# Weight-block sums of a seven-product feed-forward layer on GpSimd, result sums 512 wide

## The chip, the cores and the metric

The kernel runs on one core of a Trainium2 chip. The metric is the device time of one execution in microseconds. One core has TensorE (PE, with PEld for its weight loads), VectorE (DVE), ScalarE (ACT), GpSimd (POOL) and SyncE (SP, here the issuer of most DMAs). A comparison takes the median of several executions; the profile is one execution.

## The reference, cut to what matters

A two-layer decoder on 512 tokens of width 1024: each layer has a feed-forward block, a token mixer (latent attention in layer 0, sparse attention in layer 1) with memory attention, and a second feed-forward block, each followed by a layer norm. The change touches the four feed-forward blocks alone:

```python
D_MODEL, SEQ, D_FF = 1024, 512, 2816

def swiglu(x, w_gu, w_down):
    g, u = jnp.split(x @ w_gu, 2, axis=-1)
    return (jax.nn.silu(g) * u) @ w_down

x = layer_norm(DN_ALPHA * x + 0.5 * swiglu(x, ffn_w_gu[layer, 0], ffn_w_down[layer, 0]),
               ln_g[layer, 0], ln_b[layer, 0])
```

## The kernel before

**Arithmetic.** Every matrix product is made with float32r operands split in two: `split` (L195) casts a tile to hi on ACT (L199) and makes lo = source - hi on DVE (L200). A product is then hi x hi, hi x lo and lo x hi, so three matmuls stand for one.

**A feed-forward block** (`ffn`, L457) has 22 blocks of 128 hidden features, in five groups of four or five (`GROUPS`). An "s" is a single: gate and up are made plainly (`single`, two weight units). A "d" is a pair of gate and up made together by `seven` (L485): gate half and up half of the weights are each cut in two along the input features, the tokens in two halves of 256, and the 2 x 2 by 2 x 2 block product is made with seven quarter products instead of eight. There are 77 pairs in the four blocks (19, 19, 20 and 19). A quarter (L371) is 12 matmuls of 128x256: four hi x hi (L376), four hi x lo (L377), four lo x hi (L380).

**Weight units.** `_unit_order` lists the order in which weight tiles are used; a pair takes four units, g0 to g3, and behind each group come its down-projection units, one per hidden block. `prep` (L154) loads a unit through SP (`load`, L127) into one of four `wraw` buffers and splits it into one of seven hi/lo slots (three of `wring`, four of `W.extra`). For a pair `combined` (L133) loads only g0 (the gate weights) and g1 (the up weights, U) and makes the other operands by four 128x512 sums: two for g1 (L145, L146), one for g2 (L149), one for g3 (L151), each in place or into a third buffer. `unit` prepares up to four units ahead in program order.

**Token forms.** The quarters multiply not only token blocks but differences of them, `F.t[1]` to `F.t[4]`, made once per block by `token_forms` (L386) from raw copies b.

**Result sums.** A pair's seven quarter results lie in four PSUM banks: p12, p45, p67 and p3. One ACT copy (L495) and seven DVE sums of 128x256 (L496, L505 to L509, L513) make the gate half gs and the up half us; `evac` (L471) then takes silu on ACT, the product with 0.5 and up on DVE (L474) and the split into hhi and hlo. PSUM has eight banks, which `fbank` deals out in turn, so a bank comes round again two pairs later.

**Down projection.** `by_units` (L438) runs a group's units over two token tiles and then over the other two; it starts on the banks that have been free longest. The last group of a block goes through `token_major` (L421) instead, token tile 0 to 3 on banks 0,1 to 6,7, with residual sum (L315) and layer norm (L319) behind each tile; the norm takes its power on POOL (L328).

**What sets the order.** The program is written as a dataflow; a planner places each engine's instructions by priority and estimated time before the run, so an engine's order need not be that of the code, and it is fixed when the kernel runs. Each engine takes its instructions in that order and waits at semaphores.

Of the kernel before, what the change touches and what calls it, by code (L numbers as in the profile page):

```python
# [9 lines left out]
F32 = mybir.dt.float32  # L10
# [7 lines left out]
P = 128  # L18
# [86 lines left out]
def tile_trunk(ctx: ExitStack, tc, a: dict, out):  # L105
# [27 lines left out]
    def combined(name, idx):  # L133


        l, f, m = idx
        lo, up = slice(0, 512), slice(512, 1024)
        op = nc.vector.tensor_tensor
        if name == "g0":
            W.g = load(a["gu"][l, f, m, 0])  # L140
            return W.g
        if name == "g1":
            W.u = load(a["gu"][l, f, m, 1])
            W.s = wraw.tile([P, 1024], F32, name="wraw")
            op(W.s[:, up], W.g[:, lo], W.u[:, lo], op=ALU.subtract)  # L145
            op(W.u[:, lo], W.u[:, lo], W.u[:, up], op=ALU.add)  # L146
            return W.u
        if name == "g2":
            op(W.s[:, lo], W.u[:, lo], W.g[:, lo], op=ALU.subtract)  # L149
            return W.s  # L150
        op(W.g[:, up], W.g[:, up], W.s[:, lo], op=ALU.subtract)  # L151
        return W.g[:, up]

    def prep():  # L154
# [22 lines left out]
    def unit(name, idx, look):  # L177
        assert order[W.pos][:2] == (name, tuple(idx)), (order[W.pos], name, idx)
        if W.done <= W.pos:
            prep()  # L180
        ahead(look)
        W.pos += 1
        return W.ready.pop(W.pos - 1)
# [79 lines left out]
    def open_f(scope):  # L263
        F.st = ExitStack()
        W.extra = F.st.enter_context(tc.tile_pool(name=f"wx{scope}", bufs=NEXTRA, reuse_waits="tile"))
        F.xp = F.st.enter_context(tc.tile_pool(name=f"xp{scope}", bufs=1, reuse_waits="tile"))
        F.xp.tile([P, 112], F32, name="offset")
        F.sm = F.st.enter_context(tc.tile_pool(name=f"sm{scope}", bufs=2, reuse_waits="tile"))
        F.x = [F.xp.tile([P, D], F32, name=f"x{t}") for t in range(NT)]
        F.bk = 0  # L270
        W.scope = scope
        W.count = 0
        F.fst = ExitStack()
        F.fm = F.fst.enter_context(tc.tile_pool(name=f"fm{scope}", bufs=1, reuse_waits="tile"))
        for i in (1, 2, 3, 0, 4):
            for e in "hl":
                if i:
                    F.fm.tile([P, 4, 256], F32, tag=f"t{i}{e}", name="place")
            if not i:
                F.fm.tile([P, 80], F32, name="offset")  # L280
# [104 lines left out]

    def token_forms():  # L386

        def less(x, y):
            u = wraw.tile([P, 1024], F32, name="wraw").rearrange("p (k q) -> p k q", k=4)
            nc.vector.tensor_tensor(u, x, y, op=ALU.subtract)  # L390
            return u

        def form(i, u):
            F.t[i] = [F.fm.tile([P, 4, 256], F32R, tag=f"t{i}{e}", name="t") for e in "hl"]
            split(*F.t[i], u)

        b, F.t = F.raw, {}
        u = less(b[0, 1], b[0, 0])
        form(1, u)
        yield  # L400
        u = less(b[1, 1], u)
        form(2, u)
        yield
        u = less(u, b[1, 0])
        form(4, u)
        u = less(b[1, 1], b[0, 1])
        form(3, u)

    def prod(ps, w, a, first, last):
        (hi, lo), (ahi, alo), (p0, p1) = w, a, ps  # L410
# [46 lines left out]
    def ffn(l, f, i, halves, spill=None, final=False, mid=None, hook=None):  # L457
        hst, hp = right_pool(f"h{l}{f}")
        if hook is None:
            load_gb(l, i)  # L460
        groups = _groups(l, f)
        for gi, (m0, items) in enumerate(groups):
            n = len(items)
            hhi = hp.tile([P, 5, T], F32R, tag="hhi", name="hhi")
            hlo = hp.tile([P, 5, T], F32R, tag="hlo", name="hlo")

            def fbank():
                F.bk += 1
                return bank(F.bk - 1)

            def evac(j, pg, pu, sg=None):  # L471
                sg = sg or hp.tile([P, T], F32, tag="sg", name="sg", bufs=3)
                nc.scalar.activation(sg, pg, AF.Silu)
                nc.vector.scalar_tensor_tensor(sg, sg, 0.5, pu, op0=ALU.mult, op1=ALU.mult)  # L474
                split(hhi[:, j, :], hlo[:, j, :], sg)

            def single(j):
                pp = []
                for g in range(2):
                    w = unit("gu", (l, f, m0 + j, g), 4)  # L480
                    pp.append(fbank())
                    feature_major(w, pp[g], 0, T)
                evac(j, *pp)

            def seven(j):  # L485

                c0, c1 = slice(0, 256), slice(256, 512)
                gs = hp.tile([P, T], F32, tag="sg", name="gs", bufs=3)
                us = hp.tile([P, T], F32, tag="sg", name="us", bufs=3)
                op = nc.vector.tensor_tensor  # L490
                w = unit("g0", (l, f, m0 + j), 4)
                p12 = fbank()
                quarter(p12[:, c0], w, 0, *quarters(0, 0))
                quarter(p12[:, c1], w, 512, *quarters(1, 0))
                nc.scalar.copy(us[:, c0], p12[:, c0])  # L495
                op(gs[:, c0], us[:, c0], p12[:, c1], op=ALU.add)  # L496
                w = unit("g1", (l, f, m0 + j), 4)
                p45 = fbank()
                quarter(p45[:, c0], w, 512, *F.t[4])
                quarter(p45[:, c1], w, 0, *F.t[1])  # L500
                w = unit("g2", (l, f, m0 + j), 4)
                p67 = fbank()
                quarter(p67[:, c0], w, 0, *F.t[2])
                quarter(p67[:, c1], w, 512, *F.t[3])
                op(us[:, c0], us[:, c0], p67[:, c0], op=ALU.add)  # L505
                op(gs[:, c1], us[:, c0], p45[:, c1], op=ALU.add)
                op(us[:, c0], us[:, c0], p67[:, c1], op=ALU.add)
                op(us[:, c1], us[:, c0], p45[:, c1], op=ALU.add)
                op(us[:, c0], us[:, c0], p45[:, c0], op=ALU.subtract)  # L509
                w = unit("g3", (l, f, m0 + j), 4)  # L510
                p3 = fbank()
                quarter(p3[:, c0], w, 0, *quarters(1, 1))
                op(gs[:, c1], gs[:, c1], p3[:, c0], op=ALU.add)  # L513
                evac(j, gs, us, gs)

            j = 0
            if gi == 0:
                forms = token_forms() if halves else F.forms
            if gi == 0 and halves:
                ws, ps = [], []  # L520
                for j in range(3):
                    for g in range(2):
                        ws.append(unit("gu", (l, f, m0 + j, g), 0))
                        ps.append(fbank())
                if hook is not None:
                    hook()
                    load_gb(l, i, nc.sync)
                for c in range(2):
                    for w, p in zip(ws, ps):
                        feature_major(w, p, c * 256, c * 256 + 256)  # L530
                for j in range(3):
                    next(forms, None)
                    evac(j, ps[2 * j], ps[2 * j + 1])
                j = 3
                items = items[3:]
            for it in items:
                if gi == 0:
                    next(forms, None)
                if it == "d":
                    if gi == 0:  # L540
                        for _ in forms:
                            pass
                    seven(j)
                else:
                    single(j)
                j += 1

            last = gi == len(groups) - 1
            if gi == 2 and mid is not None:
                mid()  # L550

            def on_tile(t, ps):
                st = residual(t, ps, gi == 0, last)
                if last:
                    if t == 0 and not final:
                        new_xt()
                        if spill is None:
                            new_blocks()
                    norm_tile(t, st, spill, final)

            names = [("dn", (l, f, m0 + j)) for j in range(n)]

            def lhs(k, t):
                return hhi[:, k, t * P:(t + 1) * P], hlo[:, k, t * P:(t + 1) * P]

            if last:
                token_major(names, lhs, on_tile)
            else:
                by_units(names, lhs, on_tile, F.bk, 4)
        hst.close()  # L570
# [942 lines left out]
```

## Time and profile before

| what | value |
|---|---|
| median of 3 runs | 1869.84 us (1868.44 to 1870.9) |
| the profiled execution | 1869.39 us |
| its span, first to last instruction | 1867.5 us |
| PE, DVE, ACT, POOL busy | 1842.7, 1465.6, 869.4, 164.3 us |
| mean granted TensorE clock | 0.997 of full speed |

The span is 1.9 us shorter than the execution's own time. Busy PE means that a matmul is recorded as running; matmuls are pipelined, and the time of one as listed overlaps that of the next, so the pitch from start to start is what counts. The four feed-forward blocks lie at about 5 to 336, 568 to 880, 954 to 1267 and 1524 to 1852 us.

### The profile page before, as it was taken

How to read it: one execution, taken by the hardware profiler on the slowest of the kernel's cores; microseconds unless marked ns; L12 is line 12 of the kernel's file. 1: busy time of each engine (PE TensorE's matmuls, PEld its weight loads, DVE VectorE, ACT ScalarE, POOL GpSimd, SP SyncE). 2: the span in 40 equal slices, each digit the busy share in tenths (PEclk: the TensorE clock that was granted, in tenths of full speed). 3: DMA queues.
4: the chain of work that ended last, by engine and by line, in shares of the span. 5: the costliest groups of instructions: out<-in, count | busy, mean ns of one | idle time of the engine just before them, and what ended most of it. 6: DMA issues, size and time to landing. Idle time of an engine off the chain costs nothing.

```text
span 1867.5 us, 31922 instructions
## 1 busy us (share of the span) xinstructions
PE 1842.7 (99%) x12776; PEld 1651.6 (88%) x12776; DVE 1465.6 (78%) x2362; ACT 869.4 (47%) x1435; POOL 164.3 (9%) x185
## 2 busy tenths in 40 slices
PE   9999999999999999999999999999999999999998
PEld 8899899896679899899998998998956689999997
DVE  8798789757668789788897987987677378888887
ACT  6344345456545345334653443444566345434432
POOL 0000000025500000000100000001265100000000
PEclk9999999999999999999999999999999999999999
DMA  6333335531134234234333323343321224323322
GB/s 241 112 114 111 116 105 157 173 102 35 57 113 136 80 102 136 80 102 147 130 127 104 125 91 103 112 138 140 108 46 28 98 77 143 103 90 114 115 81 77
DMA packets 59701, 203.86 MB, mean 109 GB/s; under 512 B 6944, under 2 KB 7216, under 8 KB 59552
## 3 DMA queue, kind: packets, MB, share of 16 engines
q1 hardware_dynamic: 56848, 194.18, 31.8%
q0 software_dynamic: 2416, 7.11, 1.2%
q8 instruction: 101, 1.65, 0.4%
q10 hardware_dynamic: 288, 0.52, 0.1%
q14 instruction: 48, 0.39, 0.1%
HBM read 188.16 MB, written 7.34 MB: 105 GB/s over the span
## 4 chain that ended last, share of the span: by engine, by line
PE 89%; DVE 4%; ACT 2%; issue 2%; POOL 1%; DMA 1%; POOLq 0%; DVEq 0%; ACTq 0%
PE bank L376 13%; PE bank L380 13%; PE bank L377 13%; PE bank L415 4%; PE bank L411 4%; PE bank L413 4%; PE bank L412 4%; PE bank L414 4%; PE bank L416 4%; PE o L646 3%; PE bank L365 3%; PE bank L368 3%; PE bank L363 3%; PE tb L618 3%; PE s L1191 1%
## 5 line engine op out<-in xcount | busy, mean ns | idle before, releaser
L199 ACT CAST whi<-wraw 128x1024 fp32r<-128x1024 f32 (+3 forms) x479 | 463.4, 976 | 547.5 <-PE bank L416 246.9
L200 DVE TENSOR_TENSOR wlo<-wraw,whi 128x1024 fp32r<-128x1024 f32 (+3 forms) x479 | 536.4, 1126 | 133.7 <-ACT whi L199 132.7
L376 PE MATMUL bank<-t,whi 128*128 128x256 f32 x1232 | 298.4, 278 | 0.0
L377 PE MATMUL bank<-t,whi 128*128 128x256 f32 x1232 | 297.9, 278 | 0.0
L377 PEld LDWEIGHTS bank<-t,whi 128*128 128x128 f32 x1232 | 231.9, 188 | 0.0
L376 PEld LDWEIGHTS bank<-t,whi 128*128 128x128 f32 x1232 | 231.8, 188 | 0.0
L376 PE MATMUL bank<-xhi,whi 128*128 128x256 f32 x924 | 221.9, 277 | 0.0
L377 PE MATMUL bank<-xlo,whi 128*128 128x256 f32 x924 | 221.9, 277 | 0.0
L380 PE MATMUL bank<-t,wlo 128*128 128x256 f32 x1232 | 191.8, 278 | 0.0
L377 PEld LDWEIGHTS bank<-xlo,whi 128*128 128x128 f32 x924 | 173.6, 188 | 0.6
L376 PEld LDWEIGHTS bank<-xhi,whi 128*128 128x128 f32 x924 | 173.6, 188 | 0.6
L380 PEld LDWEIGHTS bank<-t,wlo 128*128 128x128 f32 x1232 | 164.2, 189 | 0.0
L315 DVE SCALAR_TENSOR_TENSOR x<-x,bank 128x512 f32<-128x512 f32 x176 | 112.5, 682 | 58.9 <-PE bank L415 54.4
L380 PE MATMUL bank<-xhi,wlo 128*128 128x256 f32 x924 | 142.9, 277 | 0.0
L363 PE MATMUL bank<-xhi,whi 128*128 128x256 f32 x544 | 130.7, 281 | 1.3 <-ACT xhi L199 1.3
L365 PE MATMUL bank<-xlo,whi 128*128 128x256 f32 x544 | 130.6, 281 | 1.2 <-DVE xlo L200 1.2
L412 PE MATMUL bank<-whi,hhi 128*128 128x512 f32 x336 | 131.0, 390 | 0.0
L414 PE MATMUL bank<-wlo,hhi 128*128 128x512 f32 x336 | 130.9, 390 | 0.0
L411 PE MATMUL bank<-whi,hhi 128*128 128x512 f32 x336 | 130.8, 390 | 0.0
L415 PE MATMUL bank<-whi,hlo 128*128 128x512 f32 x336 | 130.8, 389 | 0.0
L413 PE MATMUL bank<-wlo,hhi 128*128 128x512 f32 x336 | 130.8, 389 | 0.0
L416 PE MATMUL bank<-whi,hlo 128*128 128x512 f32 x336 | 130.7, 389 | 0.0
(330 smaller groups left out, 3542.3 us busy)
## 6 DMA issues: line engine op xcount, KB each, us to landing
wraw<-in_gu SPq DMA_DIRECT2D x175, 512.0 KB, 3.3
wraw<-in_dn SPq DMA_DIRECT2D x88, 512.0 KB, 3.8
wraw<-in_wo SPq DMA_DIRECT2D x16, 512.0 KB, 3.6
wraw<-in_wm SPq DMA_DIRECT2D x8, 512.0 KB, 4.2
x_dram<-x SPq DMA_DIRECT2D x8, 512.0 KB, 2.9
x<-x_dram SPq DMA_DIRECT2D x8, 512.0 KB, 4.5
wraw<-in_w SPq DMA_DIRECT2D x8, 512.0 KB, 4.6
wraw<-in_wq SPq DMA_DIRECT2D x6, 512.0 KB, 3.5
```

The lines of the kernel that those rows point to most:

```text
L199: nc.scalar.copy(hi, src)
L200: eng.tensor_tensor(lo, src, hi.bitcast(F32), op=ALU.subtract)
L363: nc.tensor.matmul(ps[:, c0:c1], lhsT=hi[:, k * P:(k + 1) * P], rhs=F.xhi[:, k, c0:c1], start=k == 0, stop=False)
L376: nc.tensor.matmul(ps, lhsT=hi[:, ks], rhs=xh[:, k], start=k == 0, stop=False)
L377: nc.tensor.matmul(ps, lhsT=hi[:, ks], rhs=xl[:, k], start=False, stop=False)
L380: nc.tensor.matmul(ps, lhsT=lo[:, ks], rhs=xh[:, k], start=False, stop=k == 3)
L411: nc.tensor.matmul(p0, lhsT=ahi, rhs=hi[:, 0:512], start=first, stop=False)
L412: nc.tensor.matmul(p1, lhsT=ahi, rhs=hi[:, 512:1024], start=first, stop=False)
L413: nc.tensor.matmul(p0, lhsT=ahi, rhs=lo[:, 0:512], start=False, stop=False)
L414: nc.tensor.matmul(p1, lhsT=ahi, rhs=lo[:, 512:1024], start=False, stop=False)
L415: nc.tensor.matmul(p0, lhsT=alo, rhs=hi[:, 0:512], start=False, stop=last)
L416: nc.tensor.matmul(p1, lhsT=alo, rhs=hi[:, 512:1024], start=False, stop=last)
```

## The change

The four weight sums of a pair move from `nc.vector` to `nc.gpsimd`, and each subtraction among them becomes an addition. To pay for the signs, token forms 1 and 2 are negated (two of the four are now made by a scalar_tensor_tensor with -x - y), and the up half of a pair comes out negated, which `evac` takes back with -0.5. The quarters are laid out anew over four banks (p15, p26, p4, p37), gate and up halves live in one tile of 128x2x512, two of which are kept where three tiles of 128x512 were, and the seven result sums of 256 become three of 512 and one of 256, with one operand read twice by broadcast. The places of the token forms in memory are reordered.

```diff
@@ combined @@
-        op = nc.vector.tensor_tensor
+        op = nc.gpsimd.tensor_tensor
...
-            op(W.s[:, up], W.g[:, lo], W.u[:, lo], op=ALU.subtract)
+            op(W.s[:, up], W.g[:, lo], W.u[:, lo], op=ALU.add)
             op(W.u[:, lo], W.u[:, lo], W.u[:, up], op=ALU.add)
             return W.u
         if name == "g2":
-            op(W.s[:, lo], W.u[:, lo], W.g[:, lo], op=ALU.subtract)
+            op(W.s[:, lo], W.u[:, lo], W.g[:, lo], op=ALU.add)
             return W.s
-        op(W.g[:, up], W.g[:, up], W.s[:, lo], op=ALU.subtract)
+        op(W.g[:, up], W.g[:, up], W.s[:, lo], op=ALU.add)
@@ open_f @@
-        for i in (1, 2, 3, 0, 4):
+        for i in (2, 3, 4, 0, 1):
@@ token_forms @@
-        def less(x, y):
+        def less(x, y, neg=False):
             u = wraw.tile([P, 1024], F32, name="wraw").rearrange("p (k q) -> p k q", k=4)
-            nc.vector.tensor_tensor(u, x, y, op=ALU.subtract)
+            if neg:
+                nc.vector.scalar_tensor_tensor(u, x, -1.0, y, op0=ALU.mult, op1=ALU.subtract)
+            else:
+                nc.vector.tensor_tensor(u, x, y, op=ALU.subtract)
...
-        u = less(b[0, 1], b[0, 0])
+        u = less(b[0, 0], b[0, 1])
         form(1, u)
         yield
-        u = less(b[1, 1], u)
+        u = less(u, b[1, 1], True)
         form(2, u)
         yield
-        u = less(u, b[1, 0])
-        form(4, u)
-        u = less(b[1, 1], b[0, 1])
-        form(3, u)
+        form(4, less(u, b[1, 0], True))
+        form(3, less(b[1, 1], b[0, 1]))
@@ ffn @@
+            def hidden():
+                return hp.tile([P, 2, T], F32, tag="sg", name="sg", bufs=2)
+
-            def evac(j, pg, pu, sg=None):
-                sg = sg or hp.tile([P, T], F32, tag="sg", name="sg", bufs=3)
+            def evac(j, sg, pg, pu, sign):
                 nc.scalar.activation(sg, pg, AF.Silu)
-                nc.vector.scalar_tensor_tensor(sg, sg, 0.5, pu, op0=ALU.mult, op1=ALU.mult)
+                nc.vector.scalar_tensor_tensor(sg, sg, 0.5 * sign, pu, op0=ALU.mult, op1=ALU.mult)
@@ seven, as it is after @@
+                both = hidden()
+                gs, us = both[:, 0], both[:, 1]
+                h = both.rearrange("p a (b q) -> p (a b) q", b=2)
...
+                p15, p26 = fbank(), fbank()
+                quarter(p15[:, c0], w, 0, *quarters(0, 0))
+                quarter(p26[:, c0], w, 512, *quarters(1, 0))
                 w = unit("g1", (l, f, m0 + j), 4)
+                p4, p37 = fbank(), fbank()
+                quarter(p15[:, c1], w, 0, *F.t[1])
+                quarter(p4[:, c0], w, 512, *F.t[4])
                 w = unit("g2", (l, f, m0 + j), 4)
+                quarter(p26[:, c1], w, 0, *F.t[2])
+                nc.scalar.copy(h[:, 2], p15[:, c0])
+                sums(h[:, 0:4:3], twice(h[:, 2]), banked(p26))
+                quarter(p37[:, c1], w, 512, *F.t[3])
                 w = unit("g3", (l, f, m0 + j), 4)
+                quarter(p37[:, c0], w, 0, *quarters(1, 1))
+                sums(h[:, 1:3], twice(h[:, 3]), banked(p37))
+                sums(h[:, 1:4:2], h[:, 1:3], twice(p15[:, c1]))
+                sums(h[:, 2], h[:, 2], p4[:, c0])
+                evac(j, gs, gs, us, -1)
```

## Rows read from the trace of the kernel before

**Rows 1.** The page, part 1: busy us, share of the span, instructions.

```profile
PE 1842.7 (99%) x12776; PEld 1651.6 (88%) x12776; DVE 1465.6 (78%) x2362; ACT 869.4 (47%) x1435; POOL 164.3 (9%) x185
```

**Rows 2.** Second feed-forward block: PE, PEld, DVE, ACT, POOL busy us (count); clock, DMA.

```profile
575.00:880.00 305.00, 305.00 (x2210) 286.90 (x2209) 254.69 (x391) 132.61 (x167) 0.00 (x0) 1.00 0.36 116
```

**Rows 3.** Waits of PE, the longest: us in total, times, longest.

```profile
PE bank L339 <- DVE x L334: 4.1, 9, 0.5
```

**Rows 4.** Timeline of PE at the end of a pair: start us, us, instruction.

```profile
322.10 0.28 PE L376 MATMUL bank<-xhi,whi 128*128 128x256 f32 x1
...
323.46 0.39 PE L411 MATMUL bank<-whi,hhi 128*128 128x512 f32 x1
...
324.83 0.40 PE L411 MATMUL bank<-whi,hhi 128*128 128x512 f32 x1
```

**Rows 5.** Groups of instructions on DVE by shape: count | busy us, mean ns | idle before.

```profile
L200 DVE TENSOR_TENSOR wlo<-wraw,whi 128x1024 fp32r<-128x1024 f32 x389 | 474.1, 1222 | 111.6 <-ACT whi L199 111.0
L200 DVE TENSOR_TENSOR wlo<-wraw,whi 128x512 fp32r<-128x512 f32 x79 | 53.9, 683 | 20.3 <-ACT whi L199 20.3
L145 DVE TENSOR_TENSOR wraw<-wraw 128x512 f32<-128x512 f32 x77 | 52.8, 686 | 9.0 <-DMA wraw<-in_gu 8.5
L505 DVE TENSOR_TENSOR us<-us,bank 128x256 f32<-128x256 f32 x77 | 32.1, 417 | 15.6 <-PE bank L380 14.1
```

**Rows 6.** Timeline of DVE within a pair, closely queued.

```profile
160.79 1.22 DVE L200 TENSOR_TENSOR wlo<-wraw,whi 128x1024 fp32r<-128x1024 f32 x1
161.93 0.41 DVE L509 TENSOR_TENSOR us<-us,bank 128x256 f32<-128x256 f32 x1
162.26 0.68 DVE L200 TENSOR_TENSOR wlo<-wraw,whi 128x512 fp32r<-128x512 f32 x1
162.86 0.68 DVE L474 SCALAR_TENSOR_TENSOR gs<-gs,us 128x512 f32<-128x512 f32 x1
```

**Rows 7.** Groups of instructions on POOL by shape, both in the attention stages.

```profile
L200 POOL TENSOR_TENSOR qt<-f,qt 128x512 fp32r<-128x512 f32 x10 | 12.8, 1281 | 4.4 <-ACT qt L199 4.4
...
L1205 POOL TENSOR_TENSOR pp<-pp,rs 128x512 f32<-128x512 f32 x12 | 12.5, 1039 | 0.0
```

**Rows 8.** L1172 by duration ns min/median/max; then DVE and POOL side by side.

```profile
L1172 DVE SCALAR_TENSOR_TENSOR rs<-rs,gt x24: 151/164/1785, 1354.0 to 1457.4; 128x4 f32<-128x4 f32 x24
...
1365.95 1.78 DVE L1172 SCALAR_TENSOR_TENSOR rs<-rs,gt 128x4 f32<-128x4 f32 x1
1365.83 1.89 POOL L1205 TENSOR_TENSOR pp<-pp,rs 128x1024 f32<-128x1024 f32 x1
...
460.73 1.23 DVE L200 TENSOR_TENSOR wlo<-wraw,whi 128x1024 fp32r<-128x1024 f32 x1
460.92 2.72 POOL L891 TENSOR_TENSOR pp<-pp,rs 128x384 f32<-128x384 f32 x2 [0.37 <-DVE rs L888]
468.01 1.82 POOL L891 TENSOR_TENSOR pp<-pp,rs 128x384 f32<-128x384 f32 x2 [1.62 <-DVE rs L888]
...
436.55 0.68 DVE L863 TENSOR_TENSOR f<-j,cs 128x512 f32<-128x512 f32 x1
436.57 1.28 POOL L200 TENSOR_TENSOR qt<-f,qt 128x512 fp32r<-128x512 f32 x1
```

**Rows 9.** Timeline of ACT: casts of weight units, with the wait before them.

```profile
167.06 1.06 ACT L199 CAST whi<-wraw 128x1024 fp32r<-128x1024 f32 x1 [1.67 <-PE bank L377]
...
171.14 0.62 ACT L199 CAST whi<-wraw 128x512 fp32r<-128x512 f32 x1 [1.66 <-DVE wlo L200]
```

**Rows 10.** The page, part 6: KB each, median us from issue to landing.

```profile
wraw<-in_gu SPq DMA_DIRECT2D x175, 512.0 KB, 3.3
```

**Rows 11.** Timeline where the last group's down projection starts, last block.

```profile
1837.57 0.72 PE L411 MATMUL bank<-whi,hhi 128*128 128x512 f32 x2
1837.77 0.42 DVE L513 TENSOR_TENSOR gs<-gs,bank 128x256 f32<-128x256 f32 x1
1838.36 0.39 PE L412 MATMUL bank<-whi,hhi 128*128 128x512 f32 x1
```

More of the change, by code (lines that the diff above doesn't have):

```diff
@@ L482, in single @@
                     feature_major(w, pp[g], 0, T)
-                evac(j, *pp)
+                evac(j, hidden()[:, 0], *pp, 1)
             def seven(j):
-                c0, c1 = slice(0, 256), slice(256, 512)
[L488 to L493, printed above, removed]
@@ L494, in seven, with sums, twice @@
-                quarter(p12[:, c1], w, 512, *quarters(1, 0))
-                nc.scalar.copy(us[:, c0], p12[:, c0])
-                op(gs[:, c0], us[:, c0], p12[:, c1], op=ALU.add)
+                both = hidden()
+                gs, us = both[:, 0], both[:, 1]
+                h = both.rearrange("p a (b q) -> p (a b) q", b=2)
+                def sums(o, x, y):
+                    nc.vector.tensor_tensor(o, x, y, op=ALU.add)
+                def twice(x):
+                    return x[:, None, :].to_broadcast([P, 2, 256])
@@ L497, in seven, with banked @@
+                def banked(p):
+                    return p.rearrange("p (b q) -> p b q", b=2)
+                w = unit("g0", (l, f, m0 + j), 4)
+                c0, c1 = slice(0, 256), slice(256, 512)
+                p15, p26 = fbank(), fbank()
+                quarter(p15[:, c0], w, 0, *quarters(0, 0))
+                quarter(p26[:, c0], w, 512, *quarters(1, 0))
                 w = unit("g1", (l, f, m0 + j), 4)
-                p45 = fbank()
-                quarter(p45[:, c0], w, 512, *F.t[4])
@@ L500, in seven @@
-                quarter(p45[:, c1], w, 0, *F.t[1])
+                p4, p37 = fbank(), fbank()
+                quarter(p15[:, c1], w, 0, *F.t[1])
+                quarter(p4[:, c0], w, 512, *F.t[4])
                 w = unit("g2", (l, f, m0 + j), 4)
[L502 to L506, printed above, removed]
@@ L507, in seven @@
-                op(us[:, c0], us[:, c0], p67[:, c1], op=ALU.add)
-                op(us[:, c1], us[:, c0], p45[:, c1], op=ALU.add)
-                op(us[:, c0], us[:, c0], p45[:, c0], op=ALU.subtract)
-                w = unit("g3", (l, f, m0 + j), 4)
[L511 to L514, printed above, removed]
+                quarter(p26[:, c1], w, 0, *F.t[2])
+                nc.scalar.copy(h[:, 2], p15[:, c0])
@@ L532, in ffn @@
                     next(forms, None)
-                    evac(j, ps[2 * j], ps[2 * j + 1])
+                    evac(j, hidden()[:, 0], ps[2 * j], ps[2 * j + 1], 1)
                 j = 3
```

## The prediction

> **What bounds the kernel now.** I read the views in this order: busy time by engine, busy time by stage, the waits of TensorE (PE), the instruction groups of VectorE (DVE) and GpSimd (POOL), and the timeline of a few pairs. The first says that PE is busy for 99% of the span [rows 1]. That alone is no proof, so the second matters more: in a feed-forward stage of 305 us PE is busy for all 305, DVE for 254.69, POOL for nothing [rows 2]; the other three such stages look the same. The third asks where PE waits: its longest entry is 4.1 us in all, at the transposes of the layer norms, outside the pairs [rows 3]. PE also runs at its pitch: from the first matmul of a quarter to the first one behind it are 12 matmuls in 1.36 us, 0.1133 us each, and six down-projection matmuls take 1.37 us [rows 4]. A pair has 7 quarters, 84 matmuls, so 9.52 us of PE. I conclude that DVE, though 84% busy there, has slack enough not to be felt, and that taking work off it can only pay where PE waits for it, which inside the pairs is nowhere.
>
> **How far ahead the weights are.** A unit's hi and lo tiles sit in seven slots (three and four), and the hi cast of a unit starts when PE has left the unit seven places earlier; the row of such a cast names exactly this wait [rows 9]. Six units lie between. For a g1 they are g3, a whole pair and a g0: 1.36 + 9.52 + 2.72 = 13.6 us, less 1.06 for the cast, so the weights are ready about 12.5 us before use. That is the cover of everything that the change makes later.
>
> **The change part by part.**
> Removed from DVE: four sums of 128x512 per pair, 0.69 us each [rows 5] and 0.60 from start to start when queued closely, as the 512-wide ones are [rows 6]: 2.40 us per pair. With 77 pairs that is 185 us of DVE, all beside PE work. On PE's path: 0.
>
> Result sums: seven of 256 at 0.33 become three of 512 at 0.60 and one of 256, 2.31 against 2.13 us [rows 6]. Saved: 0.18 us of DVE per pair, on the path 0. DVE's own work per pair falls from 9.93 (lo splits 3 x 1.14 + 0.60, product 0.60, hidden lo 0.60, sums 4.71) to 7.35.
>
> Added to POOL: four adds of 128x512. The trace has none, but two near rows: a POOL subtract of two full 128x512 operands at 1.28 us, and a multiply with a broadcast factor at 1.04 [rows 7]. The operands here are two full tensors, so I take 1.28: 5.12 us per pair, bounds 4.16 and 5.12. Nothing on POOL stands in their way: in the stage shown it executes nothing [rows 2], and the units behind the last pairs have no sums, so the layer norms' power operation finds an empty queue.
> The Trainium skill (GPSIMD Engine Reference, "Elementwise — side-by-side cycle accounting") speaks against moving such work: it gives 4497 ns for an add of 2048 on GpSimd, 1.96 times VectorE. A quarter of it, an estimate, is 1.12 us, and the four adds would take 4.5 us by it instead of 5.12.
>
> Contention: rows show DVE and POOL excluding each other. A DVE instruction on 128x4, which has a median of 164 ns, took 1.78 us when it started beside a POOL multiply, and ended as that did; the other way round, two POOL multiplies that take 1.82 us took 2.72 when a lo split had begun 0.19 us before them. A DVE product with one operand in PSUM ran its normal 0.68 us beside a POOL subtract [rows 8]. So I count as exclusive what reads two SBUF operands on DVE: lo splits, product, hidden lo, 4.02 + 1.20 = 5.22 us per pair. The result sums read PSUM and can run beside POOL.
> The Trainium skill (SBUF — State Buffer, "Who interferes with whom") states this as an exclusive lock held for the whole instruction, for a DVE operation with two SBUF inputs against a GpSimd operation that reads SBUF; the trace agrees with the 1.78 and 2.72 us above. By it the two engines' times add up, as in the next sum; with shared bandwidth instead the moved work would be free.
>
> Sum for a pair's preparation: 5.22 + 5.12 = 10.34 us if all result sums run beside POOL, 12.47 if none does. Both are over PE's 9.52, so preparation falls behind by 0.8 to 3.0 us per pair; I take the middle, 11.4, so 1.9. The first pair of a group is prepared during the down projection before it, so a group of four falls behind three times (5.7 us), one of five four times (7.6; at the upper bound 11.8). Against the cover of 12.5 us PE waits for nothing. Behind a group PE has four or five down units, 10.9 us for each two token tiles of four units (8 x 1.37), so 21.9 us in which POOL has only the next pair: the lag is made good. A group of four has 60 us of PE; even the serial demand, 4 x 12.47 + 4 x 1.14 + 8 x 0.60 = 59.2, fits. On the path: 0, with some tenths of a us of risk.
>
> New waits: the ACT cast of g1, g2 and g3 now waits for POOL; behind it on ACT stand the copy of p15, silu and the hidden cast, and behind the lo splits on DVE the result sums. They free PSUM banks, which PE needs 9.52 us (one pair) after a pair's end; with a lag of 5.7 to 7.6 us and the 1.8 us of sums (below) this still fits, narrowly. That makes it the tightest place inside a group.
>
> Bank release at a group's end: p4 and p15 are now freed only by the last sums, two of 0.69 and one of 0.42 [rows 5] after the last quarter, 1.8 us. In the last group of three feed-forward blocks (bank counter 82, remainder 2; the third block has 6) p4 is bank 0, which token tile 0 of the down projection starts on. The instruction order is not the program's: in the last block of before PE runs L411 twice before L412, whose bank is freed by the DVE sum L513 at 1837.77 [rows 11]. I expect the planner to go round the longer wait too; cost 0, at most 3 x 1.8 = 5.4 us.
>
> The rest has one answer. Two token forms of each block become scalar_tensor_tensor, which costs the same as a tensor_tensor of equal size (0.68 us for the product and for a 512-wide lo split [rows 6]); they lie beside the single units' matmuls. The 0.5 turned into -0.5, the places of the t tiles and the 2 KB more per partition for the hidden tiles cost nothing on an engine; they may shift a tile's reuse wait between stages by some tenths of a us either way.
>
> **The sum.** The profiled execution took 1869.39 us, span 1867.5 and 1.9 around it; the median of before is 1869.84. Change on PE's path: 0 plus some tenths. Forecast: 1870.0 us, its own range 1868 to 1872.
>
> **The rivals.**
> A, slower: weights come late. A weight buffer closes a loop: the up half of a pair is loaded into the buffer that the pair before frees with its last lo split. If all exclusive work of a pair falls into this loop it takes 3.3 (load [rows 10]) + 5.12 (adds) + 0.62 (cast of g3 [rows 9]) + 4.02 (lo splits) + 1.20 (product, hidden lo) = 14.3 us; if product and hidden lo fall into the load, 13.1. It decides from 9.52 + 12.5/4 = 12.6 us in the four groups of five, from 9.52 + 12.5/3 = 13.7 in the twelve of four. At 13.5 us each group of five loses 4 x 3.98 - 12.5 = 3.4 us: 14 us in all, 1884; at 14.3 it is 26 us from the groups of five and 22 from those of four, so 1918 at the far end. For it: the exclusion is shown, and the loop's DMA cannot start earlier. Against it: casts overlap adds, and the load overlaps DVE's other work.
> B, slower: PE stands at bank 0 in the three last groups for the 1.8 us worked out above: 1869.8 + 5.4 = 1875.2. For it: the sums chain is longer by 1.4 us than now. Against it: PE already goes round L513.
> C, faster: DVE, relieved by 2.6 us per pair, serves the layer norms earlier. Its price is bounded by PE's whole wait there, 4.1 us [rows 3]: 1865.7. Against it: the last group's DVE queue holds little pair work when the norms run.
>
> **How the numbers follow.** About 0.2%, 3.7 us, is what a measurement of this kernel can tell from no change. Forecast 0.65, A 0.17, B 0.10, C 0.08. Slower by more than that: A and B, 0.27; faster: C when nearly all of it is won, 0.06; the same: 0.67. The range takes in B and the lower part of A, and leaves out most of C: 1867 to 1881.
>
> **What would show it.** In the changed kernel PE should be busy for the whole of each feed-forward stage and list no wait for POOL; POOL should show 308 adds with a mean over 1.04 us, lengthened where a lo split is before them; the lo splits' mean should rise above 1.22 us; DVE's busy time should fall by less than 2.6 x 77 = 200 us, since blocked time counts as busy; the lead of the weights should shrink along a group and recover in the down projection. Wrong: PE waits at L376 or its like inside the pairs (A), or L411 waits for a DVE sum (B), or adds well below 1.04 us without any lengthening.

## The result: 1880.6 us, slower by 0.59%

| | before | after |
|---|---|---|
| median | 1869.14 us | 1880.6 us (1879.77 to 1880.82) |
| ratio, with its 95% interval | 1 | 1.0059 [1.0042, 1.0077] |
| the profiled execution | 1869.39 us | 1880.48 us |
| its span | 1867.5 us | 1878.7 us |

The change costs about 11 us. The time lies inside the stated range of 1867 to 1881 us, 0.4 us below its upper end, but that is luck. That end was set to take in B and the lower part of A, and neither happened. The forecast, 1870.0 us and no change, was not what came: the kernel is slower, and by neither of the two mechanisms that I had priced for that side.

The profile after, with the lines that answer to rows 1 and 2 (the span and the busy time by engine; then the second feed-forward block by engine, clock and DMA):

```profile
span 1878.7 us, 31943 instructions
PE 1847.1 (98%) x12776; PEld 1650.7 (88%) x12776; DVE 1383.9 (74%) x1823; ACT 866.8 (46%) x1435; POOL 683.8 (36%) x493
...
575.00:880.00 305.00, 303.83 (x2226) 285.79 (x2224) 233.60 (x255) 132.57 (x169) 127.53 (x77) 1.00 0.33 112
```

PE is not full any more: 303.83 of 305 us where it was 305.00 [rows 2]. Across the program the busy time of DVE falls by 81.7 us and that of POOL rises by 519.5 [rows 1]. The waits of PE (us in total, times, longest) say where the new gap lies:

```profile
PE bank L412 <- ACT hhi L199: 6.9, 8, 3.0
PE bank L339 <- DVE x L334: 4.4, 10, 0.5
```

The second line is the layer norms, as before [rows 3]. The first is new: eight waits of a down-projection matmul for the ACT cast of a hidden block (hhi). To see the whole price I added up, over the feed-forward stages, how much later each matmul starts than the pitch behind its predecessor allows: 0.57 us before, 12.24 after. Of that, 5.0 us are seven waits of 0.66 to 0.80 us, 3.2 us one wait in the first block at 208.8 us, and the rest mostly slower matmuls right behind these waits (1.7 us behind the long wait, about 0.25 us behind each of the others). Little moved elsewhere. Set beside before matmul by matmul (12776 in both), the last matmul of after comes 11.2 us later; the eight places make 11.7 of that, and all the rest, the attention stages included, nets to -0.5.

**One of the seven, taken apart.** The timeline of PE at the end of the second group of the last block:

```profile
1650.89 0.39 PE L412 MATMUL bank<-whi,hhi 128*128 128x512 f32 x1
...
1658.84 0.39 PE L417 MATMUL bank<-whi,hlo 128*128 128x512 f32 x1
1659.74 0.50 PE L412 MATMUL bank<-whi,hhi 128*128 128x512 f32 x1 [0.51 <-ACT hhi L199]
```

The down projection of a group of four starts at 1650.89. It runs units 0 to 2 over two token tiles first, 36 matmuls at the pitch of 1.365 us for six, so 8.2 us. Then it needs unit 3, whose other operand is the hidden block of the pair that has only just ended. From the last quarter of that pair, its result sums, silu, the product, and the hidden cast must be done within those 8.2 us: this is the cover. In before the same chain took 5.9 us. Its lines: the start of the down projection on PE, the chain on DVE and ACT, and the first use of the cast on PE:

```profile
1641.65 0.39 PE L411 MATMUL bank<-whi,hhi 128*128 128x512 f32 x1
...
1642.47 1.22 DVE L200 TENSOR_TENSOR wlo<-wraw,whi 128x1024 fp32r<-128x1024 f32 x1
1643.61 0.41 DVE L507 TENSOR_TENSOR us<-us,bank 128x256 f32<-128x256 f32 x1
...
1644.60 1.22 DVE L200 TENSOR_TENSOR wlo<-wraw,whi 128x1024 fp32r<-128x1024 f32 x1
1645.73 0.41 DVE L509 TENSOR_TENSOR us<-us,bank 128x256 f32<-128x256 f32 x1
1646.25 0.69 DVE L474 SCALAR_TENSOR_TENSOR gs<-gs,us 128x512 f32<-128x512 f32 x1
1646.97 0.62 ACT L199 CAST hhi<-gs 128x512 fp32r<-128x512 f32 x1 [1.96 <-DVE gs L474]
1649.82 0.39 PE L411 MATMUL bank<-whi,hhi 128*128 128x512 f32 x1
```

The cast ended at 1647.59, 2.2 us before PE came to it. In after it ends at 1659.69, 8.8 us behind the start (DVE, POOL and ACT of after at this place):

```profile
1649.83 1.77 DVE L200 TENSOR_TENSOR hlo<-sg,hhi 128x512 fp32r<-128x512 f32 x1
1651.53 0.68 DVE L496 TENSOR_TENSOR sg<-sg,bank 128x512 f32<-128x512 f32 x1
1652.17 1.67 DVE L200 TENSOR_TENSOR wlo<-wraw,whi 128x1024 fp32r<-128x1024 f32 x1
1653.77 0.68 DVE L496 TENSOR_TENSOR sg<-sg,bank 128x512 f32<-128x512 f32 x1
1654.37 1.71 DVE L200 TENSOR_TENSOR wlo<-wraw,whi 128x1024 fp32r<-128x1024 f32 x1
1656.00 1.13 DVE L496 TENSOR_TENSOR sg<-sg,bank 128x512 f32<-128x512 f32 x2
1657.38 1.66 DVE L477 SCALAR_TENSOR_TENSOR sg<-sg 128x512 f32<-128x512 f32 x1 [0.24 <-ACT sg L476]
...
1651.13 1.63 POOL L149 TENSOR_TENSOR wraw<-wraw 128x512 f32<-128x512 f32 x1
1652.84 2.15 POOL L151 TENSOR_TENSOR wraw<-wraw 128x512 f32<-128x512 f32 x1
1657.20 1.29 POOL L145 TENSOR_TENSOR wraw<-wraw 128x512 f32<-128x512 f32 x1 [2.20 <-DVE sg L496]
...
1659.07 0.62 ACT L199 CAST hhi<-sg 128x512 fp32r<-128x512 f32 x1 [1.73 <-DVE sg L477]
```

Between the result sums DVE runs the next pair's lo splits, as before. Beside POOL's adds each of the two lasts 1.60 and 1.63 us from start to start instead of 1.14 and 1.13, +0.46 and +0.50. The product, 0.69 us before, begins 0.18 us behind a POOL add of 1.29, which ends at 1658.49, and is done 0.55 us after that: 1.66, or +0.97. That is 1.9 of the 2.9 us; the remaining 1.0 is the later start of the sums (the hidden lo before them took 1.77 us) and their longer form, which the first experiment sizes. A lateness of 2.9 us on a slack of 2.2 leaves 0.6, about the wait of 0.67 us that PE shows here.

The trace of after holds a control of its own. Eight down projections of groups of four start this way (the last group of each block has another order), and seven of them wait. In all seven the product begins 0.03 to 0.18 us behind a POOL add and takes 1.66 to 1.81 us, and the cast ends 8.8 to 8.9 us behind the start. In the eighth, the second group of the third block, that add was itself held up by its load and began 0.39 us behind the product:

```profile
1078.73 0.69 DVE L477 SCALAR_TENSOR_TENSOR sg<-sg 128x512 f32<-128x512 f32 x1 [0.24 <-ACT sg L476]
1079.12 1.46 POOL L145 TENSOR_TENSOR wraw<-wraw 128x512 f32<-128x512 f32 x1 [2.76 <-DMA wraw<-in_gu]
```

There the product kept its 0.69 us, the cast ended 7.7 us behind the start, and PE did not wait.

### The profile page after: what moved, and what is told of

Its sections match the earlier page's. It is cut to its first block, busy times and chain, and to the rows that moved or that the text cites. A ratio compares the mean times of both kernels' runs of the same rounds, so it can differ in the third digit from the quotient of the medians.

```text
span 1878.7 us, 31943 instructions
## 1 busy us (share of the span) xinstructions
PE 1847.1 (98%) x12776; PEld 1650.7 (88%) x12776; DVE 1383.9 (74%) x1823; ACT 866.8 (46%) x1435; POOL 683.8 (36%) x493
## 4 chain that ended last, share of the span: by engine, by line
PE 85%; DVE 8%; ACT 3%; issue 2%; POOL 1%; DMA 1%; POOLq 0%; DVEq 0%; ACTq 0%
PE bank L376 12%; PE bank L377 12%; PE bank L380 12%; PE bank L412 4%; PE bank L413 4%; PE bank L416 4%; PE bank L414 4%; PE bank L415 4%; PE bank L417 4%; PE bank L365 3%; PE o L655 3%; PE bank L368 3%; PE bank L363 3%; PE tb L627 3%; DVE wlo L200 2%
## 5 line engine op out<-in xcount | busy, mean ns | idle before, releaser
L200 DVE TENSOR_TENSOR wlo<-wraw,whi 128x1024 fp32r<-128x1024 f32 (+3 forms) x479 | 626.5, 1314 | 237.6 <-ACT whi L199 235.7
L145 POOL TENSOR_TENSOR wraw<-wraw 128x512 f32<-128x512 f32 x77 | 119.9, 1557 | 607.4 <-DVE wlo L200 278.2
L376 PE MATMUL bank<-t,whi 128*128 128x256 f32 x1232 | 298.4, 278 | 0.0
L376 PEld LDWEIGHTS bank<-t,whi 128*128 128x128 f32 x1232 | 231.8, 188 | 0.0
L376 PE MATMUL bank<-xhi,whi 128*128 128x256 f32 x924 | 221.8, 277 | 0.0
L496 DVE TENSOR_TENSOR sg<-sg,bank 128x512 f32<-128x512 f32 (+1 forms) x308 | 188.8, 613 | 4.3 <-PE bank L380 1.6
L376 PEld LDWEIGHTS bank<-xhi,whi 128*128 128x128 f32 x924 | 173.6, 188 | 0.6
L151 POOL TENSOR_TENSOR wraw<-wraw 128x512 f32<-128x512 f32 x77 | 134.1, 1742 | 89.8 <-DMA wraw<-in_gu 78.0
L149 POOL TENSOR_TENSOR wraw<-wraw 128x512 f32<-128x512 f32 x77 | 140.5, 1824 | 6.0
L412 PE MATMUL bank<-whi,hhi 128*128 128x512 f32 x336 | 131.8, 393 | 6.9 <-ACT hhi L199 6.9
L416 PE MATMUL bank<-whi,hlo 128*128 128x512 f32 x336 | 131.9, 393 | 0.0
```

The lines of the kernel that those rows point to most:

```text
L149: op(W.s[:, lo], W.u[:, lo], W.g[:, lo], op=ALU.add)
L151: op(W.g[:, up], W.g[:, up], W.s[:, lo], op=ALU.add)
L200: eng.tensor_tensor(lo, src, hi.bitcast(F32), op=ALU.subtract)
L376: nc.tensor.matmul(ps, lhsT=hi[:, ks], rhs=xh[:, k], start=k == 0, stop=False)
L412: nc.tensor.matmul(p0, lhsT=ahi, rhs=hi[:, 0:512], start=first, stop=False)
L416: nc.tensor.matmul(p0, lhsT=alo, rhs=hi[:, 0:512], start=False, stop=last)
```

## Experiments

Four things could each have made the chain late: the adds on GpSimd, the new result sums, the memory attention's loads that stand in the third group of the first block, and the place at which the down projection uses the last pair. The last two are the same in before. The expectation texts number their theories themselves. In all figures below, "behind the start" means behind the start of the group's down projection, and "excess" is the sum over the feed-forward stages used above.

### The new sums without GpSimd, and GpSimd without the new sums

The first run is after with its four weight sums back on VectorE; it keeps everything else of the change (the result sums, the negated token forms, the places of the tiles, the two hidden tiles). The second is before with its four sums on GpSimd.

```diff
 # e1, on after
-        op = nc.gpsimd.tensor_tensor
+        op = nc.vector.tensor_tensor
 # e2, on before
-        op = nc.vector.tensor_tensor
+        op = nc.gpsimd.tensor_tensor
```

> The changed kernel with its four weight sums on VectorE again (as sums); the new result sums, token forms and tiles stay. Theory 1 (GpSimd's sums and VectorE's two-operand work exclude each other, and this holds up the last pair's hidden chain at a group's end): 1868 to 1871 us, no wait of TensorE for the hidden cast. Theory 2 (the regrouped result sums, three of four behind the last quarter, make the hidden chain 1.4 us longer, and that alone brings it late): the wait stays at eight places, 1876 to 1881 us.

Measured: 1870.77 us against 1868.39, ratio 1.0012 [1.0003, 1.0020]. No wait for a hidden cast; excess over the pitch 0.80 us.

> The kernel before with its four weight sums moved to GpSimd and nothing else; three of them remain subtractions. Theory 1: waits of TensorE for the hidden cast at group ends, 1873 to 1882 us. Theory 2: 1868 to 1871 us. GpSimd's subtractions and additions should each take 1.28 us where no VectorE instruction stands in their way.

Measured: 1869.67 us, ratio 1.0005 [0.9997, 1.0014]; one wait, of 0.75 us at 208.8, excess 1.43. Each half alone is nearly free. Theory 1 expected waits in the second run and theory 2 in the first, so neither is the cause by itself. Why the second is so, although its adds run on POOL, its lines at the same place show (down projection from 1643.0):

```profile
1647.80 0.69 DVE L474 SCALAR_TENSOR_TENSOR gs<-gs,us 128x512 f32<-128x512 f32 x1
1648.63 1.30 POOL L145 TENSOR_TENSOR wraw<-wraw 128x512 f32<-128x512 f32 x1 [2.35 <-DVE gs L474]
1648.52 0.62 ACT L199 CAST hhi<-gs 128x512 fp32r<-128x512 f32 x1 [2.08 <-DVE gs L474]
```

With the old sums the next burst of adds begins behind the product, which keeps its 0.69 us, and the cast ends 6.1 us behind the start. With the new sums and no adds (e1) it ends after 6.5 us, against 5.9 before: the longer sums cost about 0.6. So neither half alone reaches the 8.2 us, and both together pass it, by more than the sum of the two (0.2 and 0.6). The traces show where the excess comes from: in after the next burst of adds begins behind the last result sum, and so just ahead of the product; in e2, at all eight groups of four, it begins 0.6 us or more behind the product's start.

### Is it the reading on GpSimd, or the step through GpSimd

In this run each add is replaced by two memsets of the same output on GpSimd, which read nothing. The casts still wait for POOL, and the weight sums themselves are left out.

```diff
 # f2, on after
-        op = nc.gpsimd.tensor_tensor
+        def op(o, x, y, op):
+            for _ in range(2):
+                nc.gpsimd.memset(o, 0.0)
```

> The changed kernel with each GpSimd sum replaced by two memsets of the same output (about 1.1 us together, which read nothing from SBUF); the weight sums are left out, so the output is another. The casts still wait for GpSimd about as long as before. If the harm comes of the exclusion between GpSimd's reads and VectorE's two-operand instructions, lo splits return to 1.22 us and no wait at the hidden cast stays: 1868.5 to 1872 us. If it comes of the added step through GpSimd alone, the waits stay: 1876 to 1881 us.

Measured: 1870.54 us against 1869.07, ratio 1.0006 [0.9997, 1.0014]; excess 0.62, no wait for a hidden cast. The lo splits in after, in before with the adds on GpSimd (e2), and in this run, then the memsets; columns are count, busy us and mean ns, idle before:

```profile
L200 DVE TENSOR_TENSOR wlo<-wraw,whi 128x1024 fp32r<-128x1024 f32 x389 | 562.2, 1448 | 208.4 <-ACT whi L199 206.6
```

```profile
L200 DVE TENSOR_TENSOR wlo<-wraw,whi 128x1024 fp32r<-128x1024 f32 x389 | 542.8, 1398 | 187.2 <-ACT whi L199 186.9
```

```profile
L203 DVE TENSOR_TENSOR wlo<-wraw,whi 128x1024 fp32r<-128x1024 f32 x389 | 475.5, 1225 | 258.4 <-ACT whi L202 256.0
L140 POOL MEMSET wraw<- 128x512 f32 x616 | 307.1, 526 | 895.4 <-DVE wlo L203 670.3 <-DMA wraw<-in_gu 161.3 <-DVE t L203 51.4
```

Beside 307 us of memsets the lo splits are back at 1225 ns, as in before [rows 5], and the loss is gone. The step through POOL is free at this length; what costs is that adds which read SBUF and DVE operations with two SBUF operands exclude each other. The two memsets are shorter together (1.05 us) than one undisturbed add (1.29), and than the 1.56 to 1.82 that adds took on average in after, so the step itself was tried shorter than it is. The cast ends 5.1 us behind the start in groups of four here, against 6.5 with the adds on VectorE (e1): a DVE rid of the adds serves the chain sooner, and the contention, at up to 8.9 us in after, takes more than that away.
The Trainium skill (SBUF — State Buffer, "Who interferes with whom") says that a VectorE instruction with two SBUF inputs contends with a GpSimd instruction that reads SBUF and not with one that only writes it; the 1225 beside memsets and 1448 beside adds agree.

### Whose adds: the first or the second pair of a group

While the last pair of a group ends, POOL makes the sums of the pair behind the next boundary. These two runs put one pair's sums of groups 2 to 5 back on VectorE: the first pair's, or the second's.

```diff
 # e3, on after
-        op = nc.gpsimd.tensor_tensor
+        first = m in [m0 for m0, _ in _groups(l, f)][1:]
+        op = (nc.vector if first else nc.gpsimd).tensor_tensor
 # f3, on after
-        op = nc.gpsimd.tensor_tensor
+        second = m in [m0 + 1 for m0, _ in _groups(l, f)][1:]
+        op = (nc.vector if second else nc.gpsimd).tensor_tensor
```

> The changed kernel with the weight sums of the first pair of groups 2 to 5 of each block on VectorE, all others on GpSimd: these are the sums that fall on the end of the group before. Theory 1 in its narrow form (these sums alone do the harm): 1868 to 1871 us. Theory 1 in its wide form (the sums of the second pair of the next group, which lie behind them, hold up the product of the last pair too): some of the waits stay, 1872 to 1877 us. Theory 2: 1876 to 1881 us.

Measured: 1872.02 us, ratio 1.0017 [1.0008, 1.0025]. In the groups of four the cast now ends 6.7 to 7.0 us behind the start, and their waits are gone. In the groups of five it comes later than in after, by up to 1.9 us, presumably as DVE now has these adds to make (the group of the long wait, which shrinks, apart). One wait of 1.3 us is left, at 1010.5 us, behind a group of five, whose cast ends 12.2 us behind the start against a cover of 10.9. Sixteen of 77 pairs off GpSimd give back some seven tenths of the loss (0.17% is left of 0.59%), as the place says they should.

> The changed kernel with the weight sums of the second pair of groups 2 to 5 on VectorE, all others on GpSimd: these are the sums beside which the last pair's product (L477) took 1.66 us instead of 0.69. If that collision decides, the hidden cast at the end of groups of four comes 0.97 us earlier, 7.8 instead of 8.8 us after the down projection starts, within the 8.2 that PE leaves it: no short waits, 1869 to 1876 us (the long wait of the first block's third group may stay). If the lengthened lo splits before it count as much, short waits of 0.3 to 0.7 us stay: 1874 to 1880 us.

Measured: 1875.89 us (1871.82 to 1877.34), ratio 1.0033 [1.0020, 1.0045]. In the profile the cast ends 7.7 to 7.8 us behind the start in six of the eight groups of four (8.2 and 8.7 in the others), and the product's mean is 729 ns (838 in after):

```profile
L478 DVE SCALAR_TENSOR_TENSOR sg<-sg 128x512 f32<-128x512 f32 x77 | 56.1, 729 | 4.9 <-ACT sg L477 4.9
PE bank L413 <- ACT hhi L200: 2.0, 2, 1.6
```

Taking the second burst away gives back 1.1 us of the chain, nearly the +0.97 read off the product. The waits shrink to two, 0.57 us at 1073.3 and 1.77 at 207.3. That profile is of an execution of 1871.82 us, though, the lowest of its range, with an excess of 4.65 us. With a slack of 0.4 us small shifts may decide; where the median's other 4 us went stays open, and as the median lies in both expected ranges, the time alone decides nothing here.

### The long wait in the first block

At 208.8 us the third group, a group of five with a cover of 10.9 us, waits 3.18 us. POOL, DVE, ACT and PE of after there (the group ends at about 198):

```profile
202.19 3.52 POOL L145 TENSOR_TENSOR wraw<-wraw 128x512 f32<-128x512 f32 x1 [19.68 <-DMA wraw<-in_gu]
205.79 1.29 POOL L146 TENSOR_TENSOR wraw<-wraw 128x512 f32<-128x512 f32 x1
...
202.20 1.22 DVE L200 TENSOR_TENSOR mlo<-mr,mhi 128x1024 fp32r<-128x1024 f32 x1
203.34 1.22 DVE L200 TENSOR_TENSOR wlo<-wraw,whi 128x1024 fp32r<-128x1024 f32 x1
...
207.12 1.06 ACT L199 CAST whi<-wraw 128x1024 fp32r<-128x1024 f32 x1 [4.60 <-POOL wraw L146]
208.20 1.33 DVE L200 TENSOR_TENSOR wlo<-wraw,whi 128x1024 fp32r<-128x1024 f32 x1 [3.05 <-ACT whi L199]
209.46 1.13 DVE L496 TENSOR_TENSOR sg<-sg,bank 128x512 f32<-128x512 f32 x2
...
212.23 0.50 PE L412 MATMUL bank<-whi,hhi 128*128 128x512 f32 x1 [3.02 <-ACT hhi L199]
```

This add was made to wait for its load and then for two DVE instructions in a row; the cast waits for the add, a lo split for the cast, and the last two result sums stand behind that lo split in DVE's order. The tiles `mr` hold the input of the memory attention (memT), which `mid()` loads and splits in this group only. The two runs move that call to another group (the edit of e4 is shown):

```diff
 # e4: gi == 4; f4: gi == 0; on after
-            if gi == 2 and mid is not None:
+            if gi == 4 and mid is not None:
```

> The changed kernel with the load and split of the memory operand moved from the third group of the first block to its fifth. If the long wait of the third group (3.2 us and then half the clock) comes of the memory load delaying the next pair's up half and with it GpSimd's sums, it goes: 5 us less, 1874.5 to 1876.5 us, with seven short waits left. If it comes of the sums of a group of five alone, it stays: 1879.5 to 1881.5 us.

> The changed kernel with the memory operand's load and split at the first group of the first block instead of the third. If the memory load is what makes the third group's wait long (3.2 us and half the clock behind it, about 5 us), this wait goes or shrinks to below 1 us: 1874.5 to 1877 us. If it has nothing to do with it: 1879 to 1882 us.

Measured: late, 1879.22 us against 1868.39, ratio 1.0061 [1.0047, 1.0074]; early, 1878.53 us against 1869.07, ratio 1.0050 [1.0038, 1.0063]. In both the wait at 208.8 is gone, so the memory loads are part of it. The profile of the late place is of its slowest execution, 1884.49 us. It has a short wait at each of the eight groups of four, and a wait of 3.57 us in the last group of the first block at 330.0 us. That one is for a bank:

```profile
PE bank L413 <- DVE sg L496: 3.4, 1, 3.4
```

No add on GpSimd has a part in it, as POOL runs nothing from 318 to 340 us: the memory splits stand on DVE ahead of the result sums that free the bank. So the late place put one wait in the place of another, and its time says little of the first.

With the early place the profile has six short waits and no long one (excess 7.66 us, in an execution of 1875.2):

```profile
PE bank L412 <- ACT hhi L199: 4.6, 6, 1.4
```

Both medians missed what was expected: the late place gained nothing, and the early one gained less than its profile shows, which is of its fastest execution. Where the rest of its median went stays open. The memory loads are part of the one long wait; the short ones stay wherever the loads are put.

### The cover itself

If the chain is late by its cover alone, then a down projection that comes to the last pair later must take the loss away with every add left on GpSimd. This order uses the last unit behind all others of all four tiles, with a cover of 16.4 us for four units (6 x 2.73) and 21.8 for five. It was also made on before, to see what the order does by itself.

```diff
 # g1, on after; g2, the same on before
+        ps = {}
         for part in (tiles[:2], tiles[2:]):
-            ps = {t: pair(t) for t in part}
+            ps.update({t: pair(t) for t in part})
...
                 for t in part:
-                    prod(ps[t], ws[k], lhs(k, t), k == 0, k == n - 1)
-                    if k == n - 1:
-                        on_tile(t, ps[t])
+                    if k < n - 1:
+                        prod(ps[t], ws[k], lhs(k, t), k == 0, False)
+        for t in tiles:
+            prod(ps[t], ws[n - 1], lhs(n - 1, t), False, True)
+            on_tile(t, ps[t])
```

> The changed kernel with another order of the down projection in groups 1 to 4: the group's last unit, which alone needs the last pair's hidden tile, is multiplied behind all other units of all four token tiles instead of behind those of the first two. The time from the start of the down projection to the first use of that tile grows from 8.2 to 16.4 us in groups of four and from 10.9 to 21.8 in those of five; GpSimd's sums stay. If the whole loss lies in this tile coming too late (14.0 us at worst), no wait of TensorE for the hidden cast is left: 1868 to 1872 us. If part of it lies elsewhere (weights, banks within the pairs), 1873 us or more.

> The control: the kernel before with the same new order of the down projection. TensorE waits for nothing there now, so the order itself should be neutral: 1867.5 to 1871 us. If it came out slower than that, the same amount would have to be taken off the other run.

Measured against 1869.11: after with this order 1870.26 us, ratio 1.0008 [0.9999, 1.0017]; before with it 1870.16, ratio 1.0000 [0.9991, 1.0009]. The two lines of g1, its longest wait of PE and its lo splits:

```profile
PE bank L339 <- DVE x L334: 4.5, 10, 0.5
L200 DVE TENSOR_TENSOR wlo<-wraw,whi 128x1024 fp32r<-128x1024 f32 x389 | 572.7, 1475 | 197.8 <-ACT whi L199 197.1
```

The contention is all there, the lo splits even a little longer than in after, and the casts of groups of four still end 8.5 to 8.9 us behind the start (13.2 in the third group of the first block). Only nobody waits for them: the hidden casts have left the list of waits, and the longest is the layer norms' again. (A start 0.39 us late at 207.3 is a bank that a result sum frees.) That settles where the 11 us are. It beats neither kernel: with PE full there is nothing for the relieved DVE to give.

### How far the adds could grow inside a pair

Eight adds per pair instead of four (each of two adds made three times), to see which limit comes first inside the pairs.

```diff
 # f5, on after; the same around the sum of g2
+            for _ in range(3):
-            op(W.s[:, up], W.g[:, lo], W.u[:, lo], op=ALU.add)
+                op(W.s[:, up], W.g[:, lo], W.u[:, lo], op=ALU.add)
```

> The changed kernel with eight adds per pair on GpSimd instead of four (two of them done three times with the same result). This tests the sum of the prediction and its first rival: 5.2 us of exclusive work more per pair, so preparation takes 15.5 to 17 us per pair against TensorE's 9.5, the cover of 12.5 us is used up within two or three pairs, and TensorE waits for weights inside the pairs: 1970 to 2090 us. If exclusion matters only at the ends of groups, some 1885 to 1900 us.

Measured: 2192.3 us, ratio 1.1733 [1.1717, 1.1749], far over what I expected. Its waits of PE:

```profile
PE bank L378 <- DVE sg L498: 123.7, 29, 10.6
PE bank L414 <- ACT hhi L201: 98.4, 17, 8.4
PE bank L378 <- ACT whi L201: 2.1, 2, 1.8
```

Inside the pairs PE stands first at the PSUM banks that the result sums free (123.7 us), and hardly at the weights (2.1 us). The order in which the limits showed, from after to f5, is: hidden cast at a group's end, banks, weights. The expectation had the weights first inside the pairs.

## Where the prediction held and where it failed, point by point

**What bounds the kernel, and what DVE's relief is worth: right.** PE was full, and taking 81.7 us off DVE bought nothing: no run was faster than before. C did not happen.

**Price of an add: right.** Undisturbed 1.29 us; 1.28 was taken from the subtract of rows 7, not the 1.04 of the broadcast multiply. The estimate worked out from the Trainium skill (GPSIMD Engine Reference, "Elementwise — side-by-side cycle accounting"), 1.12, was too low; the 1.29 decides.

**Contention: right in kind.** Lo splits rose from 1222 to 1448 ns, the adds ran at means of 1557 to 1824, and DVE's busy time fell by 81.7 instead of 200 us, as the text said it would fall short. These are lines of after to set against rows 5 and 7 (count, busy us, mean ns, idle before):

```profile
L477 DVE SCALAR_TENSOR_TENSOR sg<-sg 128x512 f32<-128x512 f32 x77 | 64.5, 838 | 4.9 <-ACT sg L476 4.9
L149 POOL TENSOR_TENSOR wraw<-wraw 128x512 f32<-128x512 f32 x77 | 140.5, 1824 | 6.0
```

**The lag of the weights: right.** In the groups of five pairs the hi and lo of g0 are ready 12.6, 11.6, 9.6 and 7.5 us before use for the second to the fifth pair, where before has 12.6, 11.6, 11.4 and 11.5. The fall of about 2 us per pair (1.9 was predicted) begins a pair later than the text had it, and the lead is back at 22 us or more for the first pair of the next group. It never ran out, so A did not happen; when the adds were doubled, weights were still not the first limit.

**The failed step** is the one on new waits. It followed ACT's queue to "silu and the hidden cast", and then to the PSUM banks: "They free PSUM banks, which PE needs 9.52 us (one pair) after a pair's end". Earlier it had called the weights' 12.5 us "the cover of everything that the change makes later". At a group's end the banks are not the earliest consumer, and the weights' cover is not the one that counts. The hidden cast itself is read by the down projection 8.2 us after the pair's end, and the chain to it, at 5.9 us, had a slack of 2.2. I called the place inside a group the tightest; the tighter one was behind it. Both numbers were in the trace of before (1641.65, 1647.59 and 1649.82 above), and the cost as well: I had counted the product and the lo splits as exclusive, but put that time into the loop of the weights alone, and not onto the chain sums, silu, product, cast. With the sizes measured since, two lo splits at +0.5, a product at up to +1.0 and the longer sums at +0.6, that is 2.6 us on a slack of 2.2. Before the result only a bound was to be had: up to one add of 1.28 us on each of these three operations, 3.8 us in all. That is over the slack, so a wait should have been among the rivals.

**"POOL has only the next pair", at a group's end: right, and the harm was there.** The text booked this stretch as the one in which the lag is made good. It is also the one in which POOL's adds stand beside the only DVE work that PE waits for; e3 took exactly these adds away and most of the loss went.

**Bank release, B: right that it costs nothing.** In after no wait at the last groups' banks appears. It did appear in e4 (3.57 us at 330.0), so it is held off by the order and not impossible.

**The new result sums: free alone, not free together.** By themselves they cost no more than what I called noise (e1, 1.0012 [1.0003, 1.0020]). The working that set them at zero looked for their effect on banks; they lengthen the hidden chain by 0.6 us.

**What would show it.** The sentence "PE should be busy for the whole of each feed-forward stage" fell at once (303.83 of 305). The three signs given for a wrong prediction, L376, L411 for a DVE sum, and cheap adds, did not contain the wait that came: L412, the old L411, for an ACT cast. The signs named for POOL's adds, the lo splits, DVE's busy time and the lead of the weights came as written; e2 has them all without the loss, so they could not tell the two apart.

## What to carry to other kernels

Where an engine is full, list every consumer of a queue that you make slower, and take for each the time from the last event before it to its use: the smallest of these is the cover. Here it lay at the turn from one loop to the next, not inside the loop. Work that excludes an engine belongs on every chain that goes through that engine, not only on the one that was moved. Two edits that are free one by one can share one slack; here one cure was at the consumer, an order that uses the newest operand last.

## What the runs showed of the hardware

**Adds and splits take turns, with rare exceptions.** Of the 308 adds of after, 307 took 1.3 to 2.3 us: an undisturbed add, or one that let at most about one split pass. The one exception is the POOL add at 202.19, which began beside a DVE split and ended only behind the second of two splits that ran back to back, 3.52 us for 1.29 (lines above). At the same spot of g1, an add begun at 201.66 got in between the same two splits and took 2.15 us. The sums of the prediction let the engines take turns, and that is what they mostly do; what decides the exception no run shows.

**A wait of PE can cost more than itself.** Behind the wait of 3.18 us at 208.8 the granted clock fell (PE's own windows: busy time, clock, DMA share, GB/s):

```profile
206.00:209.00 3.00, 3.00 (x15) 1.00 0.00 0
209.00:212.00 3.00, 0.20 (x1) 1.00 0.45 156
212.00:216.00 4.00, 3.77 (x10) 0.61 0.06 18
216.00:220.00 4.00, 4.00 (x18) 0.97 0.00 0
```

With PE almost idle for the 3 us before, the clock averages 0.61 from 212 to 216: most of it is at the lower of the two levels (1.2 instead of 2.4 GHz), and PE runs 10 matmuls in 4 us where it runs 18 behind that. The pairs behind it are about 5 us late where the wait was 3.2. It does not follow every wait of this length: in e4 PE was busy for 0.40 us of the 3.80 from 330.0 to 333.8, and the granted clock was 1.00 from 333.8 to 338.0. Behind the short wait taken apart above it is 1.00 as well (1660 to 1664), and the matmuls there take 0.39 to 0.50 us.
